# Where a block of matmuls opens: plain and summed pairs, the turns, and a stage's buffers in a two-layer hybrid trunk on one core

## The chip, the cores and the metric

One NeuronCore of one Trainium2 chip runs the whole kernel; the other seven are idle. The metric is device time in microseconds (us): 2624.61 us is the median of 3 runs of the kernel before (2624.12 to 2626.24). Everything is float32 at the boundary.

## What is computed

256 tokens of width 2048 pass through two layers. Layer 0 mixes with an mLSTM group and an SSD group behind one input projection (12336 columns) and one output projection; layer 1 mixes with causal attention of 16 heads (with 256 tokens only the own block is attended). Each mixer is followed by the same feed-forward network (FFN), which is what most of the change touches:

```python
for layer in range(DEPTH):
    xn = rms_norm(x, norm_mix[layer])
    x = x + (mixer_mlstm_ssd if layer % 2 == 0 else mixer_moba)(xn, ...)
    x = x + swiglu(rms_norm(x, norm_ffn[layer]), w_gate, w_up, w_down)   # D_FF = 5632
return rms_norm(x, final_norm)

def swiglu(x, w_gate, w_up, w_down):
    return (jax.nn.silu(x @ w_gate) * (x @ w_up)) @ w_down
```

## The kernel before, in words

Weights stream from HBM once. A float32 matrix product is made of three products of `fp32r` halves: ACT casts a weight to its high half `wh`, DVE subtracts to get the low half `wl`, and PE adds wh·xh, wl·xh and wh·xl into the same PSUM bank (the three lines of `add`, L382 to L384).

**The FFN.** `ffn` (L825) goes through 11 hidden strips of 512 columns in groups of 4, 4 and 3 (the loop at L868). For a strip, `hidden` calls `block` (L369), which makes a 2x2 arrangement of outputs (two token halves by gate and up) in the four PSUM banks F[0] to F[3] (banks 0 to 3), walking over 16 K-slices of 128 rows in 8 pairs. After a group, `down` (L848) makes two blocks q=0 and q=1 with the group's hidden values as input, which go into the residual `xres`; each has 8 pairs (groups of 4) or 6 (the group of 3).

**Plain and summed pairs.** A letter of a plan string says how a pair is computed. P is plain: 4 outputs x 2 slices x 3 products = 24 matmuls of 512 columns. S is a Strassen-like form with 7 block products instead of 8: 7 x 3 = 21 matmuls. It needs sums of the activations (`activation_sums`, made ahead, at the turn of the strip) and sums of the weights (DVE L363, L364, L366), whose halves are then split too. Products 2, 3, 4 of an S pair go into F[0] to F[2]; products 1, 7, 5, 6 into four more banks E (banks 4, 5, 6, 7). After a block's last S pair, `pre` combines the E banks (ACT L414, DVE L415 to L418), and at the block's end the F banks are added (DVE L839 in `hidden`; `add_all`, L855, in `down`). A block that has no S pair reads its F banks directly. Hidden strips use PLAN_X = "SPSPSPPP" (the first strip of each FFN is all P); downs use "SPSPPPPP" (groups of 4) and "SSPPPP" (the group of 3).

**The order of the work.** The kernel is written in one order, and the compiler's scheduler makes a fixed instruction stream for each engine of it; it may take a ready instruction ahead of one that is not. `weights` (L339) runs its casts and subtractions under `tc.high_priority(offset=800)`, so they come ahead of the other work of ACT and DVE whenever their buffers are free. Buffers: `raw` has four places, `wh` and `wl` three each; an S pair takes two of each, a P pair one. `later`/`tick` (L174, L186) hold back small work (turns of finished strips, attention heads) for a number of ticks; a tick is one pair. While `held` is true nothing of it runs: `block` sets it at the start of a block with S pairs and clears it after the last S pair, since the E banks take all the banks that the turns would use (`ring["aux"]`).

**The turn.** A finished strip is turned for the next product by `transpose_split` (L215): per half, four PE transposes into one aux bank (L222), then ACT and DVE split it, and where the strip's plan needs sums, `activation_sums` (L244) makes them.

**Stages.** `open_stage` closes the buffer pools of a stage and opens the next ones on the same memory, so a tile of the new stage waits for the old tiles that lay where it is put. The kernel has the stages m (mixer), f (FFN of layer 0), a (attention and its output projection), g (FFN of layer 1). MIXER holds `wide`, then `raw`/`wh`/`wl`, then 8 `blk`; FFN holds `raw0`, `wh0`, `wl0`, `raw1`/`wh1`/`wl1`, `skh`, `gf`, `blk`. Attention uses MIXER. Between f and a stands `row_norm` (L892), the factors of the norm, with the rotary table multiplied by them (L899).

Names of blocks below: a.h0 to a.h10 are the hidden strips of layer 0's FFN, a.d0, a.d4, a.d8 its downs, b.* the same of layer 1.

## Time and profile before

| what | us |
|---|---|
| median of 3 runs | 2624.61 |
| the profiled execution's own time | 2624.31 |
| its span, first to last instruction | 2622.5 |
| PE busy (matmul) | 2582.1 |
| DVE busy | 2010.3 |
| ACT busy | 1406.8 |
| FFN of layer 0, first to last matmul of its blocks | 790.0 to 1502.7 |
| attention and its output projection | 1507 to 1894 |
| FFN of layer 1 | 1900.8 to 2611.8 |

A profile row names an engine, a line of the kernel and a tile. PE rows are matmuls, DVE and ACT rows the elementwise work, SPq rows the issue of a DMA. The view of waits sums, per engine and line, how long it sat idle and what released it; the view by windows gives each engine's busy time within stretches of the span, with the number of instructions in brackets, and the clock that TensorE was granted as a share (PEclk). A matmul's printed duration is longer than its distance to the next one, since matmuls are pipelined.

### The profile page before, as it was taken

To read this page: it belongs to the slowest core of one execution; us is meant where nothing else is said; L and a number is where in the kernel's file an instruction comes from. 1 tells how busy PE (TensorE), PEld (TensorE's weight loads), DVE (VectorE), ACT (ScalarE), POOL (GpSimd) and SP (SyncE) were. 2 spreads that over 40 slices of the span, in tenths; PEclk is the share of its full clock that TensorE was granted. 3 is DMA by queue.
4 is the path that set the end of the run, shared out by engine and by line. 5 is a ranking of instruction groups with operands and counts; after the bars stand their busy time and mean duration, and the time that the engine had idled before them with its cause. 6 is when DMAs were issued, how large, how long until landed. Compare 5 with 4: busy or idle time off the path is not lost.

```text
span 2622.5 us, 32527 instructions
## 1 busy us (share of the span) xinstructions
PE 2582.1 (98%) x12273; PEld 2154.2 (82%) x12273; DVE 2010.3 (77%) x2528; ACT 1406.8 (54%) x1878; POOL 46.8 (2%) x97
## 2 busy tenths in 40 slices
PE   8999999999999999999999899999999999999997
PEld 7888888888888888888888788888788888888886
DVE  6666777765547998899799766566569988997997
ACT  5455665665545554555456456556445545554553
POOL 2000010000000000000000000000000000000000
PEclk9999999999999999999999999999999999999998
DMA  7566676566655565656565365555565656565653
GB/s 234 170 184 185 180 232 191 168 185 216 186 169 198 194 224 173 213 184 217 177 223 186 121 192 171 176 170 160 157 229 187 221 177 210 192 209 179 222 192 121
DMA packets 254765, 496.66 MB, mean 189 GB/s; under 512 B 15704, under 2 KB 16096, under 8 KB 254352
## 3 DMA queue, kind: packets, MB, share of 16 engines
q1 hardware_dynamic: 250816, 484.57, 57.6%
q0 software_dynamic: 2896, 8.51, 1.1%
q8 instruction: 96, 1.57, 0.2%
q10 hardware_dynamic: 896, 1.52, 0.2%
q14 instruction: 61, 0.50, 0.1%
HBM read 492.39 MB, written 2.14 MB: 189 GB/s over the span
## 4 chain that ended last, share of the span: by engine, by line
PE 93%; DVE 3%; DMA 2%; issue 1%; ACT 1%; POOL 0%; SPq 0%; ACTq 0%; POOLq 0%; DVEq 0%
PE acc_f L382 14%; PE acc_f L384 14%; PE acc_f L383 14%; PE acc_w L303 11%; PE acc_a L333 8%; PE acc_a L335 8%; PE acc_a L334 8%; PE acc_w L305 5%; PE acc_e L382 3%; PE acc_e L383 3%; PE acc_e L384 3%; PE p_tr L222 2%; DVE wl L356 1%; PE p_y L762 1%; DMA raw<-in_l_ffn_down 1%
## 5 line engine op out<-in xcount | busy, mean ns | idle before, releaser
L289 DVE TENSOR_TENSOR wl<-raw,wh 128x1024 fp32r<-128x1024 f32 (+1 forms) x385 | 469.9, 1221 | 327.4 <-ACT wh L288 325.8
L354 ACT CAST wh<-raw 128x1024 fp32r<-128x1024 f32 (+1 forms) x444 | 484.2, 1132 | 415.7 <-PE acc_f L384 356.0
L356 DVE TENSOR_TENSOR wl<-raw,wh 128x1024 fp32r<-128x1024 f32 (+1 forms) x444 | 570.3, 1321 | 133.1 <-ACT wh L354 130.6
L288 ACT CAST wh<-raw 128x1024 fp32r<-128x1024 f32 (+1 forms) x385 | 403.0, 1047 | 396.1 <-PE acc_a L335 191.1
L382 PE MATMUL acc_f<-wh,x 128*128 128x512 f32 x1048 | 408.9, 392 | 5.0 <-ACT wh L354 5.0
L383 PE MATMUL acc_f<-wl,x 128*128 128x512 f32 x1048 | 409.7, 391 | 0.0
L384 PE MATMUL acc_f<-wh,x 128*128 128x512 f32 x1048 | 409.4, 391 | 0.0
L303 PE MATMUL acc_w<-xa,wh 128*128 128x512 f32 x768 | 274.5, 401 | 1.1 <-DVE xa L168 1.1
L354 ACT CAST wh<-sums 128x1024 fp32r<-128x1024 f32 x168 | 169.5, 1050 | 136.4 <-PE acc_f L384 108.8
L382 PEld LDWEIGHTS acc_f<-wh,x 128*128 128x128 f32 x1048 | 197.1, 188 | 46.9 <-ACT wh L354 5.2
L383 PEld LDWEIGHTS acc_f<-wl,x 128*128 128x128 f32 x1048 | 197.1, 188 | 40.9 <-DVE wl L356 0.8
L384 PEld LDWEIGHTS acc_f<-wh,x 128*128 128x128 f32 x1048 | 197.2, 188 | 40.6
L305 PE MATMUL acc_w<-xa,wl 128*128 128x256 f32 x768 | 215.3, 282 | 0.0
L356 DVE TENSOR_TENSOR wl<-sums,wh 128x1024 fp32r<-128x1024 f32 x168 | 198.9, 1220 | 18.2 <-ACT wh L354 17.6
L303 PE MATMUL acc_w<-x,wh 128*128 128x512 f32 x512 | 185.3, 405 | 0.0
L303 PEld LDWEIGHTS acc_w<-xa,wh 128*128 128x128 f32 x768 | 144.5, 188 | 33.1 <-ACT wh L288 1.5
L334 PE MATMUL acc_a<-wl,xa 128*128 128x512 f32 x384 | 150.2, 391 | 1.6 <-DVE wl L289 1.6
L333 PE MATMUL acc_a<-wh,xa 128*128 128x512 f32 x384 | 151.4, 394 | 0.0
L335 PE MATMUL acc_a<-wh,xa 128*128 128x512 f32 x384 | 151.1, 394 | 0.0
L305 PEld LDWEIGHTS acc_w<-xa,wl 128*128 128x128 f32 x768 | 145.4, 190 | 0.8
L305 PE MATMUL acc_w<-x,wl 128*128 128x256 f32 x512 | 143.1, 280 | 0.0
L303 PEld LDWEIGHTS acc_w<-x,wh 128*128 128x128 f32 x512 | 96.7, 189 | 22.4
(325 smaller groups left out, 4546.4 us busy)
## 6 DMA issues: line engine op xcount, KB each, us to landing
raw<-in_l_w_in SPq DMA_DIRECT2D x191, 512.0 KB, 3.6
raw<-in_l_ffn_gate SPq DMA_DIRECT2D x176, 512.0 KB, 3.9
raw<-in_l_ffn_up SPq DMA_DIRECT2D x176, 512.0 KB, 4.8
raw<-in_l_ffn_down SPq DMA_DIRECT2D x176, 512.0 KB, 5.0
raw<-in_l_w_qkv SPq DMA_DIRECT2D x96, 512.0 KB, 3.6
raw<-in_l_w_out SPq DMA_DIRECT2D x64, 512.0 KB, 4.6
raw<-in_l_w_o SPq DMA_DIRECT2D x32, 512.0 KB, 3.8
rows<-scr POOLq DMA_DIRECT2D x10, 512.0 KB, 6.2
```

What stands on the lines that cost most here:

```text
L288: nc.scalar.copy(wh[:, ks, :], raw[:, ks, :])
L289: nc.vector.tensor_sub(wl[:, ks, :], raw[:, ks, :], wh[:, ks, :].bitcast(F32))
L303: nc.tensor.matmul(banks[f], wh[:, kk, fs], kt.both(k), start=k == 0, stop=False, skip_group_check=True)
L305: nc.tensor.matmul(banks[f][:, :T], wl[:, kk, fs], kt.parts(k)[0], start=False, stop=k == nk - 1, skip_group_check=True)
L333: nc.tensor.matmul(banks[t], xh[:, ts], wh[:, kk, :], start=k == 0, stop=False)
L334: nc.tensor.matmul(banks[t], xh[:, ts], wl[:, kk, :], start=False, stop=False)
L335: nc.tensor.matmul(banks[t], xl[:, ts], wh[:, kk, :], start=False, stop=k == nk - 1)
L354: nc.scalar.copy(h[:, c, :], of[:, c, :])
L356: nc.vector.tensor_sub(l[:, c, :], of[:, c, :], h[:, c, :].bitcast(F32))
L382: nc.tensor.matmul(dst, ah, bh, start=start, stop=False)
L383: nc.tensor.matmul(dst, ah, bl, start=False, stop=False)
L384: nc.tensor.matmul(dst, al, bh, start=False, stop=stop)
```

## The change

Four things:

1. **Plans.** PLAN_X becomes "PSPSPSPP", PLAN_H "PSPSPPPP" and "PSPSPP". A block so begins with a P pair, which starts the F banks; S pairs follow with `start=False`. An S pair's products come in the order 2, 3, 1, 7, 5, 6, 4 everywhere. `held` is set at the first S pair, not at the block's start.
2. **The turns** of the previous strip therefore run right behind the first P pair of the next block (both halves at one tick), into banks 6 and 7: `turn["aux"]` is set to 0 at each block's start and the aux ring is (6, 7, 4, 5) throughout the FFN.
3. **The first strip** of each FFN uses PLAN_X too, so there are 22 blocks of hidden strips with three S pairs each instead of 20: six more S pairs.
4. **Attention.** `row_norm` and the factors on the rotary table run five ticks into the first query strip (`rope_norm`), and the stage has its own pools, ATTN: `wide` (two of twice the size), `qk` (8), `blk` (4), and then `raw`, `wh`, `wl`.

```diff
-PLAN_X = "SPSPSPPP"
-PLAN_H = {4: "SPSPPPPP", 3: "SSPPPP"}
+PLAN_X = "PSPSPSPP"
+PLAN_H = {4: "PSPSPPPP", 3: "PSPSPP"}
 MIXER = ({"wide": 2}, {"raw": 4, "wh": 3, "wl": 3}, {"blk": 8})
+ATTN = ({"wide": 2}, {"qk": 8}, {"blk": 4}, {"raw": 4, "wh": 3, "wl": 3})
 FFN = ({"raw0": 2}, {"wh0": 1}, {"wl0": 1}, {"raw1": 2, "wh1": 2, "wl1": 2}, {"skh": 2}, {"gf": 2}, {"blk": 4})
...
-    def transpose_later(kt, b, src, gcol, wait):
+    def transpose_later(kt, b, src, gcol, wait, step=1):
         for half in range(2):
-            later(wait + half, (kt.name, b), transpose_split, kt, b, src, gcol, half)
+            later(wait + half * step, (kt.name, b), transpose_split, kt, b, src, gcol, half)
...
-        last_s = plan.rfind("S")
-        held[0] = last_s >= 0
+        first_s, last_s = plan.find("S"), plan.rfind("S")
+        turn["aux"] = 0
         group = []
         for j in range(n):
             if plan[j] == "S":
+                held[0] = True
...
-                for p in (1, 7, 5, 6, 2, 3, 4) if j == 0 else (1, 2, 3, 7, 5, 6, 4):
+                for p in (2, 3, 1, 7, 5, 6, 4):
                     if p in (2, 3, 4):
                         i = p - 2
-                        if F[i] is None:
-                            F[i] = bank(i, "acc_f")
-                        add(F[i], *prod[p], start=j == 0, stop=j == n - 1)
+                        add(F[i], *prod[p], start=False, stop=False)
                     else:
                         if p not in E:
                             E[p] = bank({1: 4, 7: 5, 5: 6, 6: 7}[p], "acc_e")
-                        add(E[p], *prod[p], start=j == 0, stop=j == last_s)
+                        add(E[p], *prod[p], start=j == first_s, stop=j == last_s)
...
-            transpose_later(nx, s, [xr_[t][:, cs] for t in range(NT)], gcol, 1)
+            transpose_later(nx, s, [xr_[t][:, cs] for t in range(NT)], gcol, 1, 1 if s < 3 else 0)
...
-            transpose_later(hT, i, hs, None, 0)
+            transpose_later(hT, i, hs, None, 1, 0)
...
-        ring["aux"] = (6, 7)
+        ring["aux"] = (6, 7, 4, 5)
...
-                hidden(hT, i, first + i, PLAN_X if first + i else "P" * len(PLAN_X))
-                ring["aux"] = (4, 5, 6, 7)
+                hidden(hT, i, first + i, PLAN_X)
...
-    r2, rb2_ = row_norm("2", ss2)
...
-    nc.vector.tensor_mul(rope, rope, rb2_[:, None, :].to_broadcast([P, 2, T]))
+    norm2 = {}
+
+    def rope_norm():
+        norm2["r"], rb = row_norm("2", ss2)
+        nc.vector.tensor_mul(rope, rope, rb[:, None, :].to_broadcast([P, 2, T]))
+
+    later(5, "rope", rope_norm)
...
         banks = lin_w(w_qkv, col, xt2, KD)
-        dst = blk([P, 4, T], name)
+        need("rope")
+        dst = held_tile("qk", [P, 4, T], name)
...
-    open_stage("a", MIXER)
+    open_stage("a", ATTN)
...
-        vv = wide([P, NT, STRIP], "v4")
-        for t in range(NT):
-            nc.scalar.activation(vv[:, t, :], banks[t], AF.Copy, scale=r2[:, t:t + 1])
+        vv = wide([P, 2 * NT, STRIP], "v4")[:, :NT, :]
+        for t in range(NT):
+            nc.scalar.activation(vv[:, t, :], banks[t], AF.Copy, scale=norm2["r"][:, t:t + 1])
```

## The prediction, made before the changed kernel ran

> **What bounds the kernel now.** I read the page first, then the view of waits of PE, then windows around the waits, then the timeline of DVE at the borders of blocks. From the page:

> ```profile
> span 2622.5 us, 32527 instructions
> PE 2582.1 (98%) x12273; PEld 2154.2 (82%) x12273; DVE 2010.3 (77%) x2528; ACT 1406.8 (54%) x1878; POOL 46.8 (2%) x97
> ```

> PE is the bound, so time goes down by fewer matmuls or by the few places where PE idles. The profiled execution took 2624.31 us, 1.8 us around its span; the median of the runs is 0.3 us higher. I work from 2624.3. "Same" below means within 0.2%, about what a measurement of this kernel can tell from no change: 2619.1 to 2629.5 us.

> A matmul's price is its distance to the next. Two rows of one bank's run in the timeline, the first and the last of 24 matmuls in a row:

> ```profile
> 913.70 0.39 PE L382 MATMUL acc_f<-wh,x 128*128 128x512 f32 x1
> ...
> 918.91 0.39 PE L384 MATMUL acc_f<-wh,x 128*128 128x512 f32 x1
> ```

> (918.91 − 913.70) / 23 = 0.2265 us. A P pair is 24 of these, 5.44 us; an S pair 21, 4.76 us.

> PE's waits, those of the FFN's and attention's borders:

> ```profile
> PE acc_f L382 <- ACT wh L354: 5.0, 1, 5.0
> PE acc_e L383 <- DVE wl L356: 4.0, 2, 2.1
> PE p_tr L222 <- DVE x L168: 2.3, 1, 2.3
> PE p_tr L222 <- DVE pre L418: 2.1, 2, 1.1
> ...
> PE acc_a L334 <- DVE wl L289: 1.6, 1, 1.6
> ```

> They lie at four places, which the windows show (the column after the length is PE's busy time; PEclk is the granted clock):

> ```profile
> 138.00:146.00 8.00, 6.42 (x28) 4.95 (x27) 6.78 (x11) 2.45 (x5) 0.00 (x0) 1.00 0.41 119
> ...
> 1450.00:1462.00 12.00, 7.30 (x20) 5.18 (x21) 8.30 (x12) 1.43 (x2) 0.00 (x0) 0.72 0.26 87
> 1502.00:1510.00 8.00, 5.65 (x26) 4.58 (x26) 5.29 (x11) 6.21 (x13) 0.69 (x1) 0.79 0.17 43
> 1894.00:1906.00 12.00, 6.42 (x22) 4.42 (x21) 6.57 (x12) 6.79 (x12) 0.69 (x1) 0.72 0.93 317
> 2564.00:2575.00 11.00, 6.76 (x20) 4.88 (x20) 6.72 (x10) 0.58 (x1) 0.00 (x0) 0.69 0.28 95
> ```

> **A**, 1450 to 1462, is the turn before the last pairs of a.d8 q=0, whose plan opens with two S pairs running: 16 matmuls at 0.2265 and 4 transposes (a quarter of the columns; 0.09 each is my estimate) need 4.0 us, 12 passed: 8.0 lost. **D**, 2564 to 2575, is the same in b.d8: 15 and 4, 3.8 of 11, 7.2 lost. **B**, 1502 to 1510, is the border to attention, where `row_norm` and the last turns stand: 11 transposes, 4 matmuls of the factors and 10 others are 4.0 us at most, 4.0 lost. **C**, 1894 to 1906, the border to layer 1's FFN: 8 transposes and 13 matmuls, 3.6 of 12, 8.4 lost. Part of each loss is the clock (0.69 to 0.79 on average), not the wait. Together 27.6 us, 1.05% of the time.

> **The change part by part.**

> *Six more S pairs*: 6 x 3 matmuls x 0.2265 = **−4.1 us**. Their extra work goes to DVE, by these groups:

> ```profile
> L356 DVE TENSOR_TENSOR wl<-raw,wh 128x1024 fp32r<-128x1024 f32 x360 | 423.2, 1220 | 82.7 <-ACT wh L354 81.2
> ...
> L356 DVE TENSOR_TENSOR wl<-raw,wh 128x1536 fp32r<-128x1536 f32 x84 | 147.4, 1755 | 50.3 <-ACT wh L354 49.5
> L363 DVE TENSOR_TENSOR sums<-raw 128x1024 f32<-128x1024 f32 x84 | 102.6, 1221 | 8.1 <-DMA raw<-in_l_ffn_down 5.7 <-DMA raw<-in_l_ffn_up 1.9
> L366 DVE TENSOR_TENSOR sums<-raw,sums 128x512 f32<-128x512 f32 x84 | 57.6, 686 | 0.5
> ...
> L839 DVE TENSOR_TENSOR pre<-pre,acc_f 128x512 f32<-128x512 f32 x80 | 52.3, 680 | 0.0
> ```

> A P pair costs DVE 2 x 1.22 = 2.4 us, an S pair 1.76 + 2 x 1.22 + 1.22 + 2 x 0.69 = 6.8 us. Three S pairs and eight additions (E and F) put 3 x 4.4 + 8 x 0.68 = 18.6 us on a first strip. These windows show a first strip, a later one, and a pair of downs:

> ```profile
> 790.00:833.00 43.00, 43.00 (x192) 35.51 (x191) 30.55 (x34) 20.95 (x26) 0.69 (x1) 1.00 0.58 196
> ...
> 1132.00:1174.00 42.00, 42.00 (x191) 34.76 (x190) 40.18 (x47) 24.33 (x27) 0.00 (x0) 1.00 0.58 196
> 1217.00:1302.00 85.00, 85.00 (x381) 70.50 (x380) 72.89 (x79) 40.00 (x42) 0.00 (x0) 1.00 0.60 198
> ```

> DVE goes from 31 of 43 to about the 40 of 42 of a later strip (the rest moves behind it). PE covers that as it does there, except at the start, when no weights are ready ahead: the first S pair's sums wait for its DMA. Bounds 0 and 3 us (one S pair's DVE work less its P pair of cover), I take **+1.5 us** for both FFNs.

> *A and D.* "PSPSPP" never has two S pairs running: DVE's 6.8 us meet 4.76 + 5.44 of PE. The downs of four alternate so already, and their window has PE at 85 of 85. Lower bound of what stays 0, upper 8.0; by the nearest row, little: 1.5 each. **−6.5 − 5.7 us.**

> *B.* `row_norm` goes five ticks into the query strip. Its four small matmuls stay; its DVE and POOL chain then runs beside 5 chunks of matmuls. The other part of B is when the first weights of `w_qkv` get a place; ATTN puts `raw`, `wh`, `wl` behind 80 KB per partition, where FFN has `skh`, `gf` and the hidden values' `blk`, used by the last pairs only in part. Between 0 and 4.0 stays, 1 taken: **−3.0 us.**

> *C.* The rows of the issue queue:

> ```profile
> 1876.60 0.37 SPq L285 DMA_DIRECT2D raw<-in_l_w_o  x1
> 1894.22 0.37 SPq L347 DMA_DIRECT2D raw<-in_l_ffn_gate  x1
> ```

> and of the attention's last read of its values (first and last start):

> ```profile
> L957 PE MATMUL p_o<-pT,v x32: 272/274/275, 1597.8 to 1821.2; 128*128 128x128 f32 x32
> ```

> The first weights of layer 1's FFN are asked for 17.6 us after the last ones of the projection, at the moment when its last matmul ends: their place lies on `wh` or `wl` still in use. In ATTN, by adding up sizes, `raw0` lies on `wide`, and `wh0`, `wl0`, `raw1` on `qk`, whose attention ends at 1821. The DMA can go at 1877; the queue is not blocked by it. Between 0 and 8.4 stays, 0.7 taken: **−7.7 us.** The bank order allows it: the projection ends in banks 4 and 5.

> *P first.* This is the doubtful part. F[0] to F[3] of a block are finished 4.08, 2.72, 1.36 and 0 us before its end T. Now the next block's S pair begins with four E products, so F is needed again from T + 2.7. With P first, F[i] is needed at T + 0, 1.36, 2.72, 4.08: each has 4.08 us from its last matmul to its next. Two borders today, the first matmul of the next block and then DVE alone, a.h2 and a.h3:

> ```profile
> 919.14 0.39 PE L382 MATMUL acc_e<-wh,x 128*128 128x512 f32 x1
> ```

> ```profile
> 918.57 1.28 DVE L839 TENSOR_TENSOR pre<-pre,acc_f 128x512 f32<-128x512 f32 x2
> ...
> 920.43 2.36 DVE L356 TENSOR_TENSOR wl<-raw,wh 128x1024 fp32r<-128x1024 f32 x2
> ...
> 923.31 0.68 DVE L839 TENSOR_TENSOR pre<-pre,acc_f 128x512 f32<-128x512 f32 x1
> ...
> 924.57 0.68 DVE L839 TENSOR_TENSOR pre<-pre,acc_f 128x512 f32<-128x512 f32 x1
> ...
> 930.24 0.68 DVE L843 SCALAR_TENSOR_TENSOR h<-h,pre 128x512 f32<-128x512 f32 x1
> ```

> ```profile
> 961.76 0.39 PE L382 MATMUL acc_e<-wh,ha 128*128 128x512 f32 x1
> ```

> ```profile
> 960.78 1.88 DVE L839 TENSOR_TENSOR pre<-pre,acc_f 128x512 f32<-128x512 f32 x3
> ...
> 966.14 0.68 DVE L839 TENSOR_TENSOR pre<-pre,acc_f 128x512 f32<-128x512 f32 x1
> ```

> So T is 919.14 and 961.76. At a.h2 the third and fourth bank are free at T + 4.9 and T + 6.1, 2.1 us too late for P first; at a.h3 only the fourth, by 1.0. What holds them is the weights' `wl`, which DVE takes first. For better: the turn's splits and sums, which now stand just ahead, go behind the P pair. For worse: the E additions lie one P pair nearer. Between the last S pair's end and T + 5.44 (16.3 us) DVE would have weights 2 x 2.4 + 6.7, E and F additions 8 x 0.63, and `h` four times 0.68: 19 us, so 2.7 too much, and `h` ends near T + 8. The turn then needs 1 us until its bank is free, and the S pair needs bank 6 at about T + 8.9 (12 matmuls and the transposes after T + 5.44): just met. Sixteen borders join two hidden strips; the four that follow a strip behind a down have slack. Bounds per border 0 and 3.6 (the `h` row, T + 11.8 where T + 8.2 would do); I take 0.8, near a.h3's 1.0, at 12 borders: **+9.6 us**. The downs' additions come soon after T and pay nothing.

> Sum: −4.1 + 1.5 − 6.5 − 5.7 − 3.0 − 7.7 + 9.6 = −15.9, so **2608.4 us**.

> On the clock, the lone wait of 1.6 us in 138 to 146 left it at 1.00, while waits of at most 2.1 us close together at A brought it to 0.72. So I price single waits at borders without a clock loss. [...]

> **The rivals.**
> - *No wait at F at all*: the borders after a light strip today are all met, and the scheduler may fill a wait with the S pair's first products. 2608.4 − 9.6 = 2598.8, down to 2594 if nothing of A to D stays.
> - *The places don't clear*: if ATTN's tiles meet the last ones in use as today's do, B and C stay: 2608.4 + 10.7 = 2619.1. Against it: the sizes above.
> - *Slower: DVE gives `wl` the way at the borders*, so F, then `h`, then the turn come late and PE waits in front of the first P pair or of bank 6. Place: the 12 borders. At 2.1 us each it is at 2624, where the gain is eaten; at 3.6 us it costs 43 instead of 9.6: 2642. For it: DVE busy at 40 of 42 and 19 us of work in 16.3.
> - *The clock swings*: if each such border brought also nine matmuls at half rate (9 x 0.2265 = 2.0 us, as after A), 12 x 2.0 = 24 more: 2632. Row 138 to 146 speaks against it.

> **How the numbers follow.** Forecast (2600 to 2619) 0.50; no wait 0.12; places don't clear (2619 to 2629) 0.13; slower by DVE 0.20; by the clock 0.05. Faster 0.62, same 0.13, slower 0.25. The range from 2594 to 2640 leaves out the upper end of the DVE rival and a little below, under 2 in 10.

> **What would show it.** FFN matmuls 6066 instead of 6084. A, B, C, D: windows with PE full and clock 1.00; the first `ffn_gate` DMA right behind the last `w_o`. PE's waits at L382 for DVE L839, and at `acc_e` for ACT or DVE of the turn, give the price of P first. I am wrong if those waits exceed 25 us together, or if C's wait stays.

## The result, and the profile after

| | before | after |
|---|---|---|
| median of 4 runs (lowest to highest), us | 2624.36 (2623.65 to 2626.24) | 2668.11 (2664.26 to 2672.44) |
| the profiled execution, us | 2624.31 | 2665.1 |
| its span, us | 2622.5 | 2663.0 |
| FFN of layer 0, first to last matmul, us | 790.0 to 1502.7: 712.7 | 790.0 to 1526.3: 736.3 |
| between the FFNs, us | 398.1 | 390.8 |
| FFN of layer 1, us | 1900.8 to 2611.8: 711.0 | 1917.1 to 2652.4: 735.3 |

After to before is 1.0166 [1.0146, 1.0186]: slower by 1.7%, where faster by 0.6% was forecast, and outside the range. Two of the four runs after lie near 2665 us and two near 2672, and the profiled one is of the lower pair, so its span grew by 40.5 us where the medians differ by 43.8. The two FFNs lost 23.6 and 24.3 us; the attention between them gained 7.3.

From the page of the changed kernel, the busy time of the engines:

```profile
PE 2596.1 (97%) x12255; PEld 2146.9 (81%) x12255; DVE 2036.7 (76%) x2568; ACT 1416.9 (53%) x1886; POOL 46.8 (2%) x97
```

PE has the 18 matmuls fewer that were announced. A share of 97 instead of 98% looks like nothing: the loss is many short waits, and at some of them a halved clock (PEclk 0.50). The view of PE's waits of the changed kernel (us in total, times, the longest; the line numbers of `add` are one higher than before, L383 to L385):

```profile
PE acc_f L383 <- DVE pre L839: 29.5, 21, 1.9
PE acc_f L383 <- DVE xres L855: 5.1, 4, 2.4
PE acc_e L384 <- DVE wl L357: 4.1, 6, 1.5
...
PE p_tr L223 <- DVE x L169: 2.7, 1, 2.7
```

The first row is new. A matmul into an F bank waits until DVE has added that bank's old content to `pre`: 21 times, 1.4 us on average. The second is the same at the downs, into the residual.

Where the places A to D stand now, in windows of the changed kernel (PE's busy time after the length, PEclk the third from the end):

```profile
1484.00:1497.00 13.00, 9.26 (x28) 5.95 (x27) 10.71 (x16) 4.66 (x10) 0.00 (x0) 0.74 0.26 83
1526.00:1533.00 7.00, 4.34 (x23) 3.50 (x23) 5.44 (x12) 5.83 (x13) 0.69 (x1) 0.83 0.00 1
1915.00:1919.00 4.00, 4.00 (x20) 3.30 (x19) 1.54 (x3) 1.66 (x5) 0.00 (x0) 1.00 0.13 52
2616.00:2627.00 11.00, 8.08 (x32) 5.39 (x32) 10.93 (x16) 4.30 (x9) 0.00 (x0) 1.00 0.30 96
```

C, 1915 to 1919, is gone: PE is full. B, 1526 to 1533, is still there. A and D have moved one border on: the turn that cost them is now cheap, but the border from q=0 to q=1 of a.d8 (1484 to 1497) and of b.d8 (2616 to 2627) has a hole of its own.

Where the 40.5 us are, block by block: for each block I took the time from the start of its first matmul to 0.2265 us behind the start of its last, and subtracted 0.2265 us for each of its FFN matmuls. What remains holds the turn's transposes (about 1 us: the row of 8 at 2238.93 takes 1.03), every wait, and what a halved clock costs (matmuls 0.43 us apart instead of 0.23).

| blocks | before, us over | after, us over | change in sum |
|---|---|---|---|
| a.h0, b.h0 | 0.7, 2.4 | 2.7, 2.1 | +1.7 |
| 13 hidden strips behind a hidden strip | 1.0 to 1.7 | 2.9 to 3.8 | +25.8 |
| the other three: a.h1, b.h1, b.h5 | 1.1, 1.0, 1.0 | 7.8, 5.0, 6.3 | +16.1 |
| a.d0, a.d4, b.d0, b.d4, q=0 and q=1 | 0.9 and 0.0 | 1.8 to 3.2 and 0.0 to 0.6 | +7.5 |
| a.d8 q=0, q=1 | 9.9, 2.1 | 3.6, 9.3 | +0.9 |
| b.d8 q=0, q=1 | 8.3, 0.0 | 4.0, 4.1 | −0.2 |
| hidden strips behind a down | 0.0 | 0.0 | 0.0 |

That is +51.9; less 18 x 0.2265 = 4.1 for the matmuls saved and 7.3 for the attention, 40.5.

Now one such border, from a.h2 to a.h3. The timeline of PE in the changed kernel:

```profile
927.80 0.39 PE L383 MATMUL acc_f<-wh,x 128*128 128x512 f32 x1
...
930.97 0.39 PE L385 MATMUL acc_e<-wh,skx 128*128 128x512 f32 x1
932.75 0.50 PE L383 MATMUL acc_f<-wh,x 128*128 128x512 f32 x1 [1.39 <-DVE pre L839]
```

Here 927.80 is T, the first matmul of the new block. Nine matmuls go into F[0], which is free: six of the P pair and, by count, three of the following S pair (between T and the turn lie 27 into F banks, and a P pair has 24). Six more of the S pair go into E (`acc_e`). These nine the scheduler has put ahead. Then PE stands. The same stretch on DVE:

```profile
923.94 0.68 DVE L839 TENSOR_TENSOR pre<-pre,acc_f 128x512 f32<-128x512 f32 x1
924.54 1.75 DVE L357 TENSOR_TENSOR wl<-raw,wh 128x1536 fp32r<-128x1536 f32 x1
926.21 0.68 DVE L417 TENSOR_TENSOR pre<-pre,acc_e 128x512 f32<-128x512 f32 x1
926.80 1.21 DVE L364 TENSOR_TENSOR sums<-raw 128x1024 f32<-128x1024 f32 x1
927.94 0.68 DVE L418 TENSOR_TENSOR pre<-pre,acc_e 128x512 f32<-128x512 f32 x1
928.54 0.68 DVE L365 TENSOR_TENSOR sums<-raw,sums 128x512 f32<-128x512 f32 x1
929.14 2.35 DVE L357 TENSOR_TENSOR wl<-sums,wh 128x1024 fp32r<-128x1024 f32 x2
931.41 0.68 DVE L367 TENSOR_TENSOR sums<-raw,sums 128x512 f32<-128x512 f32 x1
932.01 0.68 DVE L839 TENSOR_TENSOR pre<-pre,acc_f 128x512 f32<-128x512 f32 x1
932.61 0.68 DVE L843 SCALAR_TENSOR_TENSOR h<-h,pre 128x512 f32<-128x512 f32 x1
933.21 0.68 DVE L839 TENSOR_TENSOR pre<-pre,acc_f 128x512 f32<-128x512 f32 x1
```

DVE never idles here. Between the first F addition and the second stand the weights of pairs that PE needs only later (L357, L364 to L367) and two E additions (L417, L418). The second F bank is free at 932.7, T + 4.9, and was wanted at T + 1.36: 3.5 us late, of which nine matmuls put ahead fill 2.0. The rest, 1.5, is what PE loses between 930.97 and 932.75 (1.78 less one distance of 0.23).

### The profile page after: what moved, and what is told of

Same layout as the page of the kernel before. It is cut to its first block, busy times and chain, and to the rows that moved or that the text cites. A ratio compares the mean times of both kernels' runs of the same rounds, so it can differ in the third digit from the quotient of the medians.

```text
span 2663.0 us, 32578 instructions
## 1 busy us (share of the span) xinstructions
PE 2596.1 (97%) x12255; PEld 2146.9 (81%) x12255; DVE 2036.7 (76%) x2568; ACT 1416.9 (53%) x1886; POOL 46.8 (2%) x97
## 3 DMA queue, kind: packets, MB, share of 16 engines
q10 hardware_dynamic: 896, 1.52, 0.2%
## 4 chain that ended last, share of the span: by engine, by line
PE 71%; DVE 16%; DMA 7%; issue 4%; ACT 2%; SPq 0%; POOL 0%; DVEq 0%; ACTq 0%; POOLq 0%
PE acc_w L304 11%; DVE wl L357 9%; PE acc_f L383 8%; PE acc_f L384 8%; PE acc_f L385 8%; PE acc_a L334 8%; PE acc_a L336 8%; PE acc_a L335 8%; PE acc_w L306 5%; DMA raw<-in_l_ffn_up 4%; DMA raw<-in_l_ffn_down 2%; ACT wh L355 2%; DVE sums L364 1%; PE p_tr L223 1%; PE acc_e L383 1%
## 5 line engine op out<-in xcount | busy, mean ns | idle before, releaser
L290 DVE TENSOR_TENSOR wl<-raw,wh 128x1024 fp32r<-128x1024 f32 (+1 forms) x385 | 469.8, 1221 | 324.7 <-ACT wh L289 323.1
L357 DVE TENSOR_TENSOR wl<-raw,wh 128x1024 fp32r<-128x1024 f32 (+1 forms) x438 | 563.6, 1329 | 119.7 <-ACT wh L355 119.7
L289 ACT CAST wh<-raw 128x1024 fp32r<-128x1024 f32 (+1 forms) x385 | 403.1, 1047 | 391.1 <-PE acc_a L336 181.4
L383 PE MATMUL acc_f<-wh,x 128*128 128x512 f32 x1012 | 397.2, 394 | 25.0 <-DVE pre L839 23.9
L384 PE MATMUL acc_f<-wl,x 128*128 128x512 f32 x1012 | 397.9, 393 | 1.3 <-DVE wl L357 1.2
L385 PE MATMUL acc_f<-wh,x 128*128 128x512 f32 x1012 | 395.9, 391 | 0.0
L355 ACT CAST wh<-sums 128x1024 fp32r<-128x1024 f32 x180 | 182.2, 1051 | 227.5 <-PE acc_f L385 89.1
L383 PEld LDWEIGHTS acc_f<-wh,x 128*128 128x128 f32 x1012 | 190.9, 189 | 72.6 <-DVE pre L839 31.1
L357 DVE TENSOR_TENSOR wl<-sums,wh 128x1024 fp32r<-128x1024 f32 x180 | 213.4, 1220 | 23.1 <-ACT wh L355 23.1
L384 PEld LDWEIGHTS acc_f<-wl,x 128*128 128x128 f32 x1012 | 191.2, 189 | 47.8 <-DVE wl L357 8.4
L385 PEld LDWEIGHTS acc_f<-wh,x 128*128 128x128 f32 x1012 | 191.1, 189 | 39.5
L334 PE MATMUL acc_a<-wh,xa 128*128 128x512 f32 x384 | 151.4, 394 | 0.0
L364 DVE TENSOR_TENSOR sums<-raw 128x1024 f32<-128x1024 f32 x90 | 109.9, 1221 | 27.2 <-DMA raw<-in_l_ffn_up 20.7
```

What stands on the lines that cost most here:

```text
L289: nc.scalar.copy(wh[:, ks, :], raw[:, ks, :])
L290: nc.vector.tensor_sub(wl[:, ks, :], raw[:, ks, :], wh[:, ks, :].bitcast(F32))
L334: nc.tensor.matmul(banks[t], xh[:, ts], wh[:, kk, :], start=k == 0, stop=False)
L355: nc.scalar.copy(h[:, c, :], of[:, c, :])
L357: nc.vector.tensor_sub(l[:, c, :], of[:, c, :], h[:, c, :].bitcast(F32))
L383: nc.tensor.matmul(dst, ah, bh, start=start, stop=False)
```

## The experiments

My theory after the result: DVE has time for all its work at a border, but its fixed order puts the coming weights ahead of the additions that empty the banks, and a P pair in front makes PE wait for that order. Rivals: DVE has too much work in that stretch (the 19 us in 16.3 of the prediction); the early turn is in the way; the S pairs in the first strips cost it. Each run stands against the kernel before on the same chip.

| run | kernel | median (before), us | ratio |
|---|---|---|---|
| E1 | before + the attention part | 2624.18 (2626.65) | 0.9987 [0.9977, 0.9996] |
| E2 | before, downs of three "SPSPPP" | 2629.67 (2626.65) | 1.0008 [0.9999, 1.0018] |
| E3 | before, first strips with S pairs | 2630.41 (2626.65) | 1.0011 [1.0002, 1.002] |
| E4 | after, E and F additions first | 2609.54 (2626.65) | 0.993 [0.9916, 0.9945] |
| E5 | after, hidden strips' turns one pair later | 2684.4 (2626.68) | 1.022 [1.0205, 1.0235] |
| E6 | after, first strips all P | 2666.03 (2626.68) | 1.0152 [1.0137, 1.0167] |
| E7 | before, E and F additions first | 2621.59 (2626.68) | 0.9981 [0.9971, 0.9991] |
| E8 | before + attention part + S pairs in first strips, additions first | 2614.92 (2626.68) | 0.9956 [0.9942, 0.9971] |
| E9 | after, only F additions first | 2629.65 (2627.62) | 1.0006 [0.9997, 1.0016] |
| E10 | after, only E additions first | 2673.17 (2627.62) | 1.0171 [1.0155, 1.0186] |
| E11 | E4, first strips all P | 2616.98 (2627.62) | 0.9957 [0.9943, 0.9972] |
| E12 | E4, the downs' `pre` into the residual first too | 2604.92 (2626.59) | 0.9919 [0.9901, 0.9937] |

### E4: the additions ahead of the weights

```diff
+                    with tc.high_priority(offset=2000):
                         nc.scalar.copy(p1, E[1])
                         nc.vector.tensor_add(v, p1, E[6])
                         ... (the other E additions)
...
+                        with tc.high_priority(offset=2000):
                             nc.vector.tensor_add(p, p, f)      # hidden
...
+                with tc.high_priority(offset=2000):
                     add_all(F)                                 # down
```

> The changed kernel with the additions that empty the E and F banks at a higher priority than the weights, so that DVE takes them first. Theory (DVE takes the weights first and F[1] comes free 3.5 us too late): PE's waits for DVE at acc_f fall from 35 to under 10 us and the time from 2668 to 2625 to 2645. Rival (DVE has too much work at a border in any order): the waits move to the weights (acc_f and acc_e waiting for wl or wh) and the time stays at 2655 to 2675.

2609.54 us, 15 below the range of the theory: the same operations in another order (on DVE, and ACT's one copy) are worth 58.6 us by the medians, and turn 1.7% slower into 0.7% faster. In its view of PE's waits no row names `pre`; these are the first that belong to the blocks and to B:

```profile
PE p_tr L223 <- DVE x L169: 2.2, 1, 2.2
PE acc_f L383 <- DVE xres L857: 1.7, 1, 1.7
PE acc_f L384 <- DVE wl L357: 1.3, 2, 0.9
```

DVE at the same border in E4, where T is 919.23:

```profile
916.71 0.69 DVE L841 TENSOR_TENSOR pre<-pre,acc_f 128x512 f32<-128x512 f32 x1
...
917.92 1.75 DVE L357 TENSOR_TENSOR wl<-raw,wh 128x1536 fp32r<-128x1536 f32 x1
919.59 1.28 DVE L841 TENSOR_TENSOR pre<-pre,acc_f 128x512 f32<-128x512 f32 x2
...
921.38 1.22 DVE L357 TENSOR_TENSOR wl<-sums,wh 128x1024 fp32r<-128x1024 f32 x1
```

The last two F additions now run in one piece and end at 920.9, T + 1.6, and `wl` of the sums comes behind them. DVE does as much as in the changed kernel (2039.4 us busy against 2036.7) in 56 us less of span: too much work was not the cause. The hidden strips fall from about 3.0 us over their matmuls' time to 1.2 to 1.7, and a.d8 q=0 and b.d8 q=0 to 1.3 and 1.2: A and D are gone as well.

### E9 and E10: one half of it each

E9 puts only the two F edits of E4 first, E10 only the E edit.

> The changed kernel with the additions of the F banks alone ahead of the weights; those of the E banks stay behind them. Theory (F is what PE waits for; v and w are ready just before T or 0.8 us after it even now, so only the F additions' own place matters): waits for pre at acc_f fall under 10 us, 2610 to 2628 us. Rival (the E additions, on which the F additions build, hold them): 2640 to 2668.

> The changed kernel with the additions of the E banks alone ahead of the weights; those of the F banks stay behind them. Theory: the F additions still stand behind the subtractions of the weights, waits for pre at acc_f stay above 20 us, 2645 to 2670. Rival (E was the hold-up): 2610 to 2630.

E9 gains 38.5 of the 58.6 us. Its time lies just above what was expected; its waits:

```profile
PE acc_f L383 <- DVE pre L840: 9.9, 14, 1.5
```

An F addition in `hidden` adds to the `pre` that the E additions make, so one that goes first still waits for them; that is what the E edit adds, some 20 us. E10 alone gains nothing: at 2673.17 it lies 3 us above the theory's range, and its waits are not those of the theory:

```profile
PE acc_e L383 <- ACT wh L355: 14.2, 21, 0.9
PE acc_e L384 <- DVE wl L357: 12.0, 11, 1.3
PE acc_f L383 <- ACT wh L355: 8.6, 28, 0.9
```

I had expected over 20 us of waits for `pre` to stay. Instead PE meets the weights, and the time is about the same. The lateness is still there: at the border from a.h2 to a.h3 (T = 927.92 in E10) the last two F additions start at 936.21, behind the weights. So I read the new names on the waits as the scheduler having put other products in front; that reading was not tested by itself.

### E7: the same order in the kernel before

The edit of E4, on the kernel before.

> The kernel before with the additions of the E and F banks ahead of the weights, nothing else of the change. Theory (its F banks are covered by the E products, so only the borders of the downs of three, where the waits for wl and the E banks came from DVE's order, can gain): 2612 to 2622 us. Rival (the order of DVE was the whole matter and opening with a plain pair brings nothing): 2603 to 2610, as the changed kernel with the same edit (2609.5). Third: the weights come late and it is slower, above 2630.

5.1 us by the medians. Late additions were there all along, but the four E products at a block's start covered them. E7 also bears on A, D and C:

```profile
PE acc_f L382 <- ACT wh L354: 4.8, 1, 4.8
...
PE acc_f L384 <- DVE hb L165: 3.4, 1, 3.4
PE acc_f L384 <- DVE ha L165: 3.4, 1, 3.4
```

C's 4.8 us stay, and at a.d8 and b.d8 PE waits 3.4 us each for the split of the strip that was turned last (`ha`, `hb`).

### E2 and E5: what A and D were

```diff
-PLAN_H = {4: "SPSPPPPP", 3: "SSPPPP"}
+PLAN_H = {4: "SPSPPPPP", 3: "SPSPPP"}
```

> The kernel before with SPSPPP instead of SSPPPP for the downs of three, nothing else. Theory (two summed pairs running were the cause of the waits at 1450 and 2566): 2610 to 2616 us. Rival (these waits come from the short block, in which the work of DVE and the weights' DMA don't fit whatever the order, and only move to the next border, as they did in the changed kernel): 2620 to 2627.

```diff
-            transpose_later(hT, i, hs, None, 1, 0)
+            transpose_later(hT, i, hs, None, 2, 0)
```

> The changed kernel with the turns of the hidden strips behind the block's last summed pair, as before, and everything else of the change. Theory (the additions of the F banks wait behind the weights on DVE; the place of the turn is secondary): waits for pre at acc_f stay near 30 us, time 2655 to 2675. Rival (the early turn makes the additions and h urgent and holds the E banks): the waits fall by half or more, 2630 to 2645.

E2 takes away the two S pairs running that I blamed, and gains nothing (1.0008, where 2610 to 2616 us was expected); it keeps 3.0 us of `PE acc_f L384 <- DVE hb L165`, and a.d8 q=0 and b.d8 q=0 go from 9.9 and 8.3 us over to 11.6 and 11.2. It does not separate the two causes fully, since its last S pair, and with it the turn, comes one pair later. E5 keeps the new plan, but lets the hidden strips' turns come behind the last S pair: a.d8 q=0 goes to 16.1 us over its matmuls and b.d8 q=0 to 15.1, and the time to 2684.4, more than expected. Its waits:

```profile
PE acc_f L383 <- DVE pre L839: 13.4, 18, 1.4
PE p_tr L223 <- DVE pre L418: 11.8, 2, 6.1
```

Those for `pre` halve instead of staying, which my theory did not have, and others take their place. E7 gives the shares with the old plan: once the additions are first, the waits for the `wl` of the second S pair (`PE acc_e L383 <- DVE wl L356: 2.6, 2, 1.3`) are 1.3 us each, and those for the late turn 3.4. So A and D come in the main from the late turn of the group's last strip, whose values the down's last pairs read; the spacing of the S pairs without the early turn does not cure them. The old spacing with an early turn was not run. The early turn is also not what costs: without it the kernel is slower.

### E3, E6, E11: the S pairs of the first strips

```diff
-                hidden(hT, i, first + i, PLAN_X if first + i else "P" * len(PLAN_X))
+                hidden(hT, i, first + i, PLAN_X)
```

E3 is this in the kernel before; E6 and E11 are the reverse in the changed kernel and in E4.

> The kernel before with summed pairs in the first strips too (SPSPSPPP there), nothing else. Theory (18 matmuls less, DVE keeps up but for the start): 2619 to 2623 us. Rival (the six summed pairs overload DVE at the start of each FFN and are part of what the change lost): 2626 to 2635.

> The changed kernel with the first strip of each FFN all plain again. Theory: 18 matmuls more (4.1 us), less DVE work at the start (the large waits behind the first strips, 7.8 and 5.0 us over the matmuls' own time, shrink), so 2662 to 2672, the same within the noise. Rival (the six summed pairs are a main part of the loss): 2640 to 2655.

> The changed kernel with both additions ahead of the weights (2609.5 us) and the first strips plain again, which takes the six summed pairs out and moves the turn of the weights' buffers by three units. Theory (a summed pair saves what it should once DVE is in order, less the start): 2 to 5 us more, 2611 to 2615. Rival (the start of each FFN, where 3.0 and 2.1 us over the matmuls' own time are lost, eats the gain): 2607 to 2610.

E3 is 0.11% slower, in the rival's range and not in the theory's: with a block that begins with S, the sums of the first weights come late (`PE acc_e L382 <- ACT wh L354: 8.5, 6, 2.9`). E6 differs from the changed kernel by less than the intervals (1.0152 and 1.0166), so the S pairs are not the cause of the loss, and hardly a gain beside it. With the additions first they gain: E11 is 7.4 us behind E4 by the medians (2 us more than expected; the kernel before was 1.0 us slower beside it). The 4.1 us of matmuls are in that, and the 3.1 us of a wait that E4 does not have:

```profile
PE acc_f L383 <- ACT wh L355: 3.4, 2, 3.1
```

### E1 and E8: the attention part

E1 is point 4 of the change alone; E8 adds to it the S pairs of E3 and the order of E4, with the old plans and turns.

> The kernel before with the attention part of the change alone (its own pools, the factors five ticks later). Theory (the loss sits at the F banks of blocks that open with a plain pair; the attention part is a gain by itself): the wait of 5.0 us at 1900 goes, 2614 to 2619 us. Rival (the new buffers only shift the wait into the attention or the next block): 2622 to 2627.

> All of the change but the plans and the turns (blocks open with a summed pair as before), and the additions of the banks ahead of the weights: against the changed kernel with that edit (2609.5 us) it has the opening alone undone. Theory (with the banks emptied in time, opening with a plain pair is worth the waits at the downs of three and at the start of each FFN): 2614 to 2624. Rival (the opening is worth nothing): 2606 to 2612.

E1 gains 2.5 us; it misses the 2614 to 2619 us that I expected and lies in the rival's range. C's wait falls from 5.0 to 3.1 us, and B's stays at 2.2:

```profile
PE acc_f L383 <- ACT wh L355: 3.1, 1, 3.1
```

The DMA of the first pair's `ffn_gate` weights went at 1878.47, right behind the last `w_o`, so the buffers did what they were for; but ACT's cast came at 1899.29, behind the residual's sums of squares and the turn's splits. E6 and E11, whose first strips are plain, have the same 3.1; the changed kernel, E4 and E8, whose first strips have S pairs, do not. The traces show the difference: in E1, E6 and E11 ACT casts the first pair 1.1 us before the FFN's first matmul, in the changed kernel, E4 and E8 68 to 69 us before it. By the count in `weights`, the S pairs of layer 0's first strip move the first pair of layer 1 from the buffer `raw1` to `raw0` (177 units taken before it instead of 174, in a ring of four). That this is what lets it go early is likely, but no run changed it alone. E8 at 2614.92 is the kernel without the new opening; E4 is 5.4 us faster, and that is what the opening, plans and turns together, is worth once the order is right. E8 still has both 3.4 us waits for `ha` and `hb`.

### E12: the residual too

In E4 the one large rest is a.d8 q=1, 5.7 us over. DVE there, in E4:

```profile
1465.35 2.35 DVE L357 TENSOR_TENSOR wl<-sums,wh 128x1024 fp32r<-128x1024 f32 x2
...
1468.22 0.69 DVE L857 TENSOR_TENSOR xres<-xres,pre 128x512 f32<-128x512 f32 x1
...
1469.42 0.68 DVE L857 TENSOR_TENSOR xres<-xres,acc_f 128x512 f32<-128x512 f32 x1
```

The F addition was first in rank, but it adds to an `xres` to which `pre` has to be added before, and that stood behind the weights.

```diff
+                        with tc.high_priority(offset=2000):
                             after_sums(pre)
```

> The changed kernel with the additions of the E and F banks ahead of the weights (2609.5 us), and the downs' additions of pre to the residual as well, since a down's F addition writes the same residual after them. Theory (at the border of the last two downs of layer 0 an F addition still stands behind one of pre, which stands behind the weights; 1.7 us of wait and 5.7 us over the matmuls' time): that wait goes, 2602 to 2608 us. Rival (that border waits for the weights' DMA and sums whatever DVE does first): 2608 to 2613.

2604.92 us, as expected: 4.6 below E4, and a.d8 q=1 at 2.2 us over. No single wait at the borders of blocks is over 1 us in its view of waits; B is the largest that is left once the kernel has its first inputs:

```profile
PE p_tr L223 <- DVE x L169: 2.9, 1, 2.9
PE acc_f L384 <- DVE wl L357: 1.1, 2, 0.7
```

It is faster than both kernels, by 0.8% against the one before.

## Why the prediction was wrong, step by step

| step | predicted, us | measured, us |
|---|---|---|
| six more S pairs | −4.1 | −4.1 |
| their start | +1.5 | +1.7 (a.h0, b.h0) |
| A, a.d8 | −6.5 | +0.9 |
| D, b.d8 | −5.7 | −0.2 |
| B and C | −10.7 | −7.3 (all between the FFNs) |
| P first | +9.6 | +49.4 |
| sum | −15.9 | +40.5 |

**The step that failed is "P first".** It was priced at 0.8 us at 12 borders. Measured are 41.9 us at all 16 borders between hidden strips (2.0 us each on average at 13 of them, 4.0 to 6.7 at a.h1, b.h1 and b.h5) and 7.5 at the four pairs of downs of four: 49.4. Of this some 6 us are a halved clock at a.h1, b.h1 and b.h5 (my estimate; see the other rivals). The terms of the working were right: the kernel before showed the third bank free at T + 4.9 behind `wl`, and in the changed kernel the second is free at T + 4.9, also behind `wl`. Three choices made it small. I took 0.8 near a.h3's 1.0 and not a.h2's 2.1, although a.h2 is the border of two hidden strips and a.h3's is one to a down. I gave the four strips behind a light one slack, and they pay: a.h5's first wait for `pre` is 1.60 us. And I let the downs pay nothing.

The slower rival named the place, the mechanism and the view in which it shows; its price of 3.6 us at 12 borders was 43, near the 49.4 partly by luck, since the price of a border was too high (2.6 on average) and the borders too few (16, and the downs). It stayed at 2642 since it kept the gains of A to D. Its argument was half wrong: not the 19 us of work in 16.3 but the order of that work (E4). The bound that I set myself, waits at L383 for L839 over 25 us together, was passed with 29.5.

**A and D** failed in their cause. I read two S pairs running; spacing them gains nothing in E2, and E5, E7 and E8 show the late turn. The early turn does cure both (E4: 1.3 and 1.2 us over), but in the changed kernel the residual's additions at the next border took the gain back: q=0 fell by 6.2 and 4.3, q=1 rose by 7.2 and 4.1.

**B** failed: its wait is 2.7 us (2.3 before), and 2.2 to 2.9 in the runs with the attention part. It is for the split of the last turn (`x`), which the later `row_norm` doesn't touch. **C** held, in the changed kernel: the first weights of layer 1's FFN are asked for at 1842.32, 75 us before its first matmul and ahead of 19 of the projection's own loads, ACT casts them at 1847.85, and the wait is gone. The issue and the cast:

```profile
1842.32 0.46 SPq L348 DMA_DIRECT2D raw<-in_l_ffn_gate  x1
```

```profile
1847.85 1.05 ACT L355 CAST wh<-raw 128x1024 fp32r<-128x1024 f32 x1
```

That is earlier than predicted, and not by the buffers alone: by E1 the attention part by itself is worth a third of it. **The S pairs** held by count, and their start at the first strip; E11 shows that they pay only when the banks are emptied in time.

**The other rivals.** "No wait at F" is refuted: the scheduler did fill the wait with S products, nine matmuls or 2.0 us at the border shown, against 3.5 us of lateness. "The clock swings" came true at three borders. The mean granted clock is 0.994 in both kernels, but that hides where it was lost: before, at A to D (0.69 to 0.79); in the changed kernel in 1484 to 1497 (0.74), at B (0.83), and at a.h1, b.h1 and b.h5, the three strips that stand out in the table; in both, also behind the last matmul (0.50 from 2615.01 and from 2657.04 on). The windows cut to these stretches, then one of a lone border, a.h5's, which keeps 1.00:

```profile
837.73:844.56 6.83, 5.51 (x13) 3.82 (x13) 6.79 (x11) 1.44 (x2) 0.00 (x0) 0.50 0.46 154
1967.55:1970.96 3.41, 3.41 (x11) 2.60 (x10) 2.36 (x5) 1.63 (x2) 0.00 (x0) 0.50 0.37 143
2233.78:2237.20 3.42, 3.42 (x10) 2.67 (x9) 3.10 (x5) 0.73 (x1) 0.00 (x0) 0.50 0.72 275
...
1102.00:1110.00 8.00, 6.40 (x30) 4.74 (x29) 7.17 (x10) 1.80 (x4) 0.00 (x0) 1.00 0.40 131
```

In these stretches matmuls start 0.43 us apart instead of 0.23. With 0.2 us lost for each of some 30 matmuls that is about 6 us, my estimate, where the rival had 24; so my pricing of borders without a clock loss held at 13 of 16. The 21 waits at F banks for `pre` came with a halved clock at three borders of hidden strips only, and only b.h1's follows a wait for a bank alone (1.92 us): just ahead of a.h1's stand waits of 0.50 and 1.52 us for weights, and ahead of b.h5's one of 1.04 for weights and one of 1.60 for a bank.

## What to carry to other kernels

Before the opening of a block is moved, list for each bank when it is last written, when it is next needed, and what stands between in the emptying engine's fixed order; cover that is not written down anywhere, here four products into other banks, goes with the move. Emptying a bank on which PE will wait should rank ahead of preparing weights for later pairs, and so should every operation that it depends on: the same work in another order was worth 58.6 us here and 5.1 where the cover still stood. When two rows give the price of a border, take the row of the border of the same kind, and count the borders by where the need arises rather than by where the slack was.

## What the runs showed of the hardware

Idle time counted within steps of 3.413 us from these starts fits better than single waits: between the same two times, four of the five stretches follow a step in which PE waited 1.92 to 2.66 us, and none starts after a step with 1.60 us or less, except the one of 1489.68 (1.35 us). The wait of 2.20 us lies across two steps, 1.46 us of it in the first. This is one execution of one kernel; no run changed the idle time alone, so what sets the clock was not shown.
